# Five pairs of split-weight buffers and seven raw slots in place of three and eleven

## The chip, the cores and the metric

The kernel runs on one core of a Trainium2 chip. The metric is the time of one execution on the device in microseconds (us); of each kernel the median of several runs is given. A profiled execution has a span and a trace of every engine: PE (TensorE, matmuls), DVE (VectorE), ACT (ScalarE), POOL (GpSimd) and SP (SyncE, which issues the loads).

## The reference

One layer of a hybrid backbone over 512 latent tokens of 1024 features (and 256 context tokens): a mixer of a bidirectional state-space scan and a pooling group, an output projection, and then a mixture of 32 experts of which each token takes four. The change lies in the last part.

```python
logits = (xt @ router_w + router_b).astype(jnp.float32)
top_val, top_idx = lax.top_k(logits, TOP_K)            # 4 of 32
gates = jax.nn.softmax(top_val, axis=-1)
...
def run_block(args):
    toks, e = args
    hb = x_pad[toks] @ w1[e] + b1[e]                   # 1024 -> 2048
    g_part = jnp.minimum(hb[..., ::2], SWIGLU_LIMIT)
    u_part = jnp.clip(hb[..., 1::2], -SWIGLU_LIMIT, SWIGLU_LIMIT)
    act = g_part * jax.nn.sigmoid(SWIGLU_ALPHA * g_part) * (u_part + 1)
    return act @ w2[e] + b2[e]                         # 1024 -> 1024
...
x = x + g2 * moe_ffn(...)
return rmsnorm(x, final_norm_w)
```

All of it is float32. w1 and w2 of all experts are 384 MB.

## The kernel before, in words

**Splitting.** A float32 product is made of products of rounded parts. A piece of weights of 1024 KB (`raw`, 128 partitions of 2048 numbers) is loaded by SP (line 1064), rounded by ACT into `hi` (line 1076), and the remainder `lo` = raw - hi is taken by DVE (line 1077). PE then multiplies (`prod`, line 1305): the rounded activations with hi, their remainder with hi, and the rounded activations with lo. For an expert with more than 64 token slots these are twelve matmuls of 512 columns a piece. Where 64 slots do, the rounded and the remaining rows lie side by side in one operand, and there are eight.

**Pieces.** The experts are sorted by load into 32 positions p. From p = 2 on, even positions hold a big expert (128 slots falling to 80; p = 16 has two blocks) and odd ones from p = 3 a small one (64 slots). Each expert has eight pieces of w1 and four of w2; there are 384 pieces, numbered here from 0. PE takes w1 of position p in pieces 12p-4 to 12p+3, and then the four of w2 of position p-1. So the last piece of w1 of p = 10 is number 123, and that of p = 11 is 135. Where a big expert's w1 ends is called a big end here, where a small one's ends a small end.

**Between w1 and w2.** When the last product of w1 is done, PE adds the bias (line 1289 for big, 1287 for small experts; the small ones' bias product needs `b2h`, a copy that ACT makes of w1's sums, line 1276). Then ACT takes the sigmoid product `sg` (line 1314), DVE clips into `su` (line 1319) and multiplies into `act` (line 1320), twice, for two halves. PE transposes `act`, and ACT and DVE split the result (`ah`, `al`). `y` (line 1326) is an expert's result; POOL adds it to the sum in DRAM.

**Buffers.** `ring` lists the slots that raw pieces take in turn: seven of the pool `pcat`, two of `strm`, two of `pm`, which comes in when the router's tiles are given up: eleven. `hring` lists the pairs for hi and lo: two in `strm` and one in `pcat` (tag `hl`): three. Before the experts begin, the same memory of `pcat` holds the transposed heads `cat`, five tiles of 1024 KB of which the first three serve the first pair of token blocks and have tag `raw`.

**Order.** A scheduler places each instruction in its engine's program before the run. Each engine works its program off in that order: what stands behind a waiting instruction waits as well. How the scheduler orders su and act against the splits of later pieces is therefore settled before the run.

Of the kernel before, what the change touches and what calls it, by code (L numbers as in the profile page):

```python
# [6 lines left out]
F32R = mybir.dt.float32r  # L7
# [9 lines left out]
P = 128  # L17
D = 1024
KT = D // P
# [78 lines left out]
def mixer_and_moe(tc, a):  # L98
# [18 lines left out]
    strm = tc.alloc_tile_pool(name="strm", bufs=1, side="right")  # L117
# [17 lines left out]
    acc_scr = dram.tile([T, D], F32, name="acc_scr")  # L135
# [29 lines left out]
    halfneg = cst.tile([P, 8], F32, name="halfneg")  # L165
# [5 lines left out]
    phx = tc.alloc_tile_pool(name="phx", bufs=1, side="right", reuse_waits="tile")  # L171
# [64 lines left out]
    for k in range(KT):  # L236
        for h in range(2):
# [7 lines left out]
            with tc.issue_after(wdma.ins):  # L245
                if 2 * k + h in (5, 9):
                    j = k // 2 - 1
# [414 lines left out]
    cat = [([None] * 4, [None] * 4) for _ in range(2)]  # L662
# [120 lines left out]
    pcat = tc.alloc_tile_pool(name="pcat", bufs=1, side="left", reuse_waits="tile")  # L783

    for i, ts in enumerate(cat):
        for j in range(3 + i):
            t = pcat.tile([P, 2, 4, 2 * P], F32R, name=f"cat{i}{j}", tag="raw", bufs=RC)
            ts[0][j], ts[1][j] = t[:, 0], t[:, 1]
    for c in (2, 3):
        pool_cat(c)  # L790
# [36 lines left out]
    strm = tc.alloc_tile_pool(name="strm2", bufs=1, side="right", reuse_waits="tile")  # L827
    phx = tc.alloc_tile_pool(name="phx2", bufs=1, side="right", reuse_waits="tile")
# [216 lines left out]
    turn = [0, 0]  # L1045
    loads = [0]
    own = [(strm, SR)]
    ring = [(pcat, RC)] * 3 + [(strm, SR)] * SR + [(pcat, RC)] * (RC - 3)
    hring = [(strm, "hi", "lo", SH)] * SH + [(pcat, "hl", "hl", 2)]

    def after(i, j, how, why):
        tc.add_manual_dep(i.ins, j.ins.name, mybir.DependencyInfo(how, mybir.DependencyReason.DATA), reason=why)
# [75 lines left out]
    xgs = [pc.tile([P, D], F32, name=f"xg{i}") for i in range(2)]  # L1128
    for t in xgs:
        PO.memset(t, 0.0)  # L1130
    lead = []
# [10 lines left out]
    for pr in range(2):  # L1142
# [7 lines left out]
        for c in cs_:  # L1150
            route(c)
            normed(c)
            table(c)

    psa = moe(tc, a, c_, cst, psa, psb, phx, pc, pd, g2, b1h, b2h, msum[:, NT - 1, :], gate, rkm, tab, *first[0], table_out,
              acc_scr, halfneg, ring, ring_raw, ring_load, ring_split, w1_piece, w1_pair, w2_pair, gather, transposed, xgs,
              lead)
    pc.release()
    phx.release()
# [27 lines left out]
RAW, HLB = 6, 3  # L1187


RC = 7  # L1190
SR = 2
RX = 2
SH = 2
# [7 lines left out]


def moe(tc, a, c_, cst, psa, psb, phx, pc, pd, g2, b1h, b2h, msum, gate, rkm, tab, ixa, last, table_out, acc_scr, halfneg,
        ring, raw, load, split, w1_piece, w1_pair, w2_pair, gather_, transposed_, xgs, lead):
    nc = tc.nc
    SC, VE, PO, PE, SP = nc.scalar, nc.vector, nc.gpsimd, nc.tensor, nc.sync
    ident = c_("ident")
# [16 lines left out]
    pd.release()  # L1224
    pm = tc.alloc_tile_pool(name="pm", bufs=1, side="right", reuse_waits="tile")
    ring += [(pm, RX)] * RX
    psa.release()
    psa = tc.alloc_tile_pool(name="psa2", bufs=1, space=PSUM, side="left", reuse_waits="tile")

# [371 lines left out]
    def half(dt_=F32):  # L1601

        if not spare.get(dt_):
            t = raw()
            t = t if dt_ is F32 else t.bitcast(dt_)
            spare[dt_] = [t[:, 0:D], t[:, D:]]
        return spare[dt_].pop(0)

    marks = half(F32R)
    place = marks[:, 0:NT * P].rearrange("p (c t) -> p c t", c=NT)  # L1610
    unit = marks[:, NT * P:(NT + 1) * P]
    for c in range(NT):
# [42 lines left out]
    i = None  # L1655
    for c in range(NT):
        for j in range(2):
            for t in (yh, yl):
# [4 lines left out]
                i = x  # L1663
# [19 lines left out]
    with tc.For_i(0, nf, 1) as _:  # L1683
# [38 lines left out]
        for c in range(NT):  # L1722
            t = half()
# [32 lines left out]
```

## Time and profile before

| | |
|---|---|
| runs | 1802.0, 1802.69, 1810.48 us; median 1802.69 |
| profiled execution | 1804.47 us, its span 1802.7 us |
| mean granted clock of PE | 0.964 |
| PE busy | 1635.2 us (91%) |
| DVE busy | 1541.8 us (86%) |
| ACT busy | 1168.1 us (65%) |
| POOL busy | 621.0 us (34%) |
| read from memory | 508.78 MB, 292 GB/s over the span |

The profiled execution is 1.8 us above the median. Of its span the weights of the experts take the stretch from about 580 to 1765 us. Shares over the whole span mix the mixer, the router and the experts; what the change touches is read from the experts' stretch.

### The profile page before, as it was taken

The page shows a single profiled execution, that of the slowest core. Times are in us where ns is not written, and L with a number is a line of the kernel's source. Part 1 is how long each engine was busy: PE and PEld are TensorE (multiplying, and loading weights), DVE is VectorE, ACT ScalarE, POOL GpSimd, SP SyncE. Part 2 cuts the span into 40 slices and gives each one's busy share as a digit, 9 for nine tenths or more (in the row PEclk, how much of TensorE's full clock was granted, in tenths as well). Part 3 has the DMA queues.
Part 4 walks back from the last instruction along what each step waited for, and adds up shares of the span by engine and source line. Part 5 has one row for each costly group of instructions (what it writes and reads, how often), then busy time and mean ns, then how long its engine had stood idle before and what let it go on. Part 6 is the DMA issues. An engine that isn't in the chain of part 4 may idle for free. (4 is left out here: it accounts for less than half of the span.)

```text
span 1802.7 us, 21388 instructions
## 1 busy us (share of the span) xinstructions
PE 1635.2 (91%) x7371; PEld 1197.1 (66%) x7371; DVE 1541.8 (86%) x1491; ACT 1168.1 (65%) x1204; POOL 621.0 (34%) x288
## 2 busy tenths in 40 slices
PE   6998889998899799999999999998999998999985
PEld 2776667676677577767667667676666666666653
DVE  7767888987878989999989998966899999999994
ACT  6445336556643467787777877755778777787773
POOL 1303456779210102242540531501053363313303
PEclk8999899999999889999999999999999999999996
DMA  9646443223577779999999999985899999999953
GB/s 350 200 127 206 150 154 105 101 82 106 191 249 304 258 289 365 363 388 384 362 388 392 356 380 401 351 304 197 341 385 384 380 365 365 390 374 374 384 222 102
DMA packets 138561, 521.53 MB, mean 289 GB/s; under 512 B 14919, under 2 KB 45063, under 8 KB 106704
## 3 DMA queue, kind: packets, MB, share of 16 engines
q1 hardware_dynamic: 125446, 490.39, 71.6%
q0 software_dynamic: 6880, 16.79, 4.0%
q10 hardware_dynamic: 6122, 12.94, 2.1%
q8 instruction: 59, 0.97, 0.2%
q14 instruction: 54, 0.44, 0.1%
HBM read 508.78 MB, written 18.37 MB: 292 GB/s over the span
## 5 line engine op out<-in xcount | busy, mean ns | idle before, releaser
L1077 DVE TENSOR_TENSOR lo<-raw,hi 128x2048 fp32r<-128x2048 f32 x398 | 897.4, 2283 | 88.5 <-ACT hi L1076 85.5
L1076 ACT ACTIVATE hi<-raw 128x2048 fp32r<-128x2048 f32 x398 | 752.0, 1915 | 180.7 <-PE A L1305 106.7
L1328 POOL DMA_INDIRECT acc_scr<-y,ixi x32 | 239.9, 7498 | 531.2 <-DVE y L1326 450.8
L1305 PE MATMUL A<-lo,xh 128*128 128x512 f32 (+3 forms) x1072 | 310.9, 407 | 37.5 <-DVE lo L1077 32.8
L1305 PE MATMUL A<-hi,xh 128*128 128x512 f32 (+3 forms) x1072 | 304.4, 400 | 7.0 <-ACT hi L1076 3.8
L1305 PEld LDWEIGHTS A<-lo,xh 128*128 128x128 f32 (+3 forms) x1072 | 184.3, 181 | 126.9 <-DVE lo L1077 80.0
L1305 PEld LDWEIGHTS A<-hi,xh 128*128 128x128 f32 (+3 forms) x1072 | 192.2, 182 | 62.8 <-ACT hi L1076 5.6
L1099 POOL DMA_INDIRECT xg<-h_scr,ixi x30 | 114.7, 3823 | 269.4 <-PE S L1109 150.2
L1305 PE MATMUL S<-lo,ah 128*128 128x512 f32 (+3 forms) x512 | 165.8, 404 | 15.4 <-DVE lo L1077 15.3
L1305 PE MATMUL S<-hi,ah 128*128 128x512 f32 (+3 forms) x512 | 165.6, 403 | 3.8 <-DVE ah L1112 3.8
L1305 PE MATMUL A<-hi,xl 128*128 128x512 f32 (+3 forms) x544 | 153.8, 396 | 0.0
L1305 PEld LDWEIGHTS S<-lo,ah 128*128 128x128 f32 (+3 forms) x512 | 90.5, 183 | 49.8 <-DVE lo L1077 24.2
L1305 PEld LDWEIGHTS A<-hi,xl 128*128 128x128 f32 (+3 forms) x544 | 95.0, 175 | 31.4
L1305 PEld LDWEIGHTS S<-hi,ah 128*128 128x128 f32 (+3 forms) x512 | 92.6, 184 | 33.2 <-DVE ah L1112 4.0
L228 ACT ACTIVATE hi<-raw 128x1024 fp32r<-128x1024 f32 (+1 forms) x73 | 75.9, 1045 | 40.0 <-PE A L355 14.3
L231 DVE TENSOR_TENSOR lo<-raw,hi 128x1024 fp32r<-128x1024 f32 (+1 forms) x59 | 77.8, 1322 | 18.6 <-ACT hi L228 17.4
L1305 PE MATMUL S<-hi,al 128*128 128x512 f32 (+3 forms) x272 | 86.2, 396 | 0.0
L630 ACT ACTIVATE row<-row,nb 128x128 f32<-128x128 f32 x192 | 59.5, 389 | 37.4 <-POOL row L626 37.3
L336 PE MATMUL A<-hx,hi 128*128 128x512 f32 x160 | 65.8, 411 | 3.4 <-DVE at L378 2.1
L338 PE MATMUL A<-hx,lo 128*128 128x512 f32 x160 | 66.2, 414 | 0.0
L337 PE MATMUL A<-hx,hi 128*128 128x512 f32 x160 | 65.2, 408 | 0.0
L378 DVE SCALAR_TENSOR_TENSOR at<-A,cw,at 128x510 f32<-128x510 f32 (+1 forms) x80 | 57.8, 740 | 5.9 <-ACT at L374 5.4
(452 smaller groups left out, 2476.1 us busy)
## 6 DMA issues: line engine op xcount, KB each, us to landing
raw<-in_w_dram SPq DMA_DIRECT2D x384, 1024.0 KB
raw<-in_w_in_dram SPq DMA_DIRECT2D x36, 512.0 KB
mraw<-in_w_mod_dram SPq DMA_DIRECT2D x32, 512.0 KB
raw<-in_w_out_dram SPq DMA_DIRECT2D x14, 1024.0 KB
row<-cs_scr ACTq DMA_DIRECT2D x32, 384.0 KB
raw<-in_w_mod_dram SPq DMA_DIRECT2D x16, 512.0 KB
raw<-in_w_in_dram SPq DMA_DIRECT2D x16, 384.0 KB
xt<-in_x_dram SPq DMA_DIRECT2D x4, 512.0 KB
```

Of the source, the lines that this page charges most:

```text
L228: SC.activation(hi, r, AF.Copy)
L231: e.tensor_tensor(lo, r, hi.bitcast(F32), op=ALU.subtract)
L336: PE.matmul(lat, lhsT=hi[:, k, :], rhs=row_of(hxh, k), start=(k == 0), stop=False)
L337: PE.matmul(lat, lhsT=hi[:, k, :], rhs=row_of(hxl, k), start=False, stop=False)
L338: newest[0] = PE.matmul(lat, lhsT=lo[:, k, :], rhs=row_of(hxh, k), start=False, stop=(k == KT - 1))
L378: VE.scalar_tensor_tensor(ac[:, u:v], src[:, u + o:v + o], cw[:, j, ct:ct + 1], ac[:, u:v], op0=ALU.mult, op1=ALU.add)
L630: SC.activation(row[:, h, :], row[:, h, :], AF.Exp, bias=nb[:, c, i:i + 1])
L1076: ia = SC.activation(hi, r, AF.Copy)
L1077: i = VE.tensor_tensor(lo, r, hi.bitcast(F32), op=ALU.subtract)
L1099: PO.indirect_dma_start(out=t[0:m, :], out_offset=None, in_=h2_scr, in_offset=bass.IndirectOffsetOnAxis(ap=col[0:m, :], axis=0), bounds_ch ...
L1305: PE.matmul(bk[0:n, :], lhsT=u[:, k, 0:n], rhs=v[:, j * 512:(j + 1) * 512], start=(k == 0 and i == 0), stop=((last or m == LT and k == KT ...
L1328: PO.indirect_dma_start(out=acc_scr, out_offset=bass.IndirectOffsetOnAxis(ap=icol[0:m, :], axis=0), in_=y[0:m, :], in_offset=None, bounds_ ...
```

## The change

The second pair's transposed heads (`cat1`, four tiles) get a tag of their own, `hq`, with four slots, and the raw slots in `pcat` go from seven to three, so the memory is the same. When the experts begin, `hring` is extended by two entries that take hi and lo from the four `hq` slots: five pairs in place of three. The ring of raw slots has five entries until `pm` comes in (nine before) and seven then (eleven before). `marks`, which serves the final sum, moves from a half of a raw slot to the tile `al`. Line numbers after the first edit move by one to four: 1077 becomes 1079, 1076 becomes 1078, 1319 becomes 1323, 1320 becomes 1324, 1314 becomes 1318.

```diff
--- before.py
+++ after.py
@@ -784,7 +784,8 @@
 
     for i, ts in enumerate(cat):
         for j in range(3 + i):
-            t = pcat.tile([P, 2, 4, 2 * P], F32R, name=f"cat{i}{j}", tag="raw", bufs=RC)
+            tag, n = (("raw", RC), ("hq", HQ))[i]
+            t = pcat.tile([P, 2, 4, 2 * P], F32R, name=f"cat{i}{j}", tag=tag, bufs=n)
             ts[0][j], ts[1][j] = t[:, 0], t[:, 1]
     for c in (2, 3):
         pool_cat(c)
@@ -1045,8 +1046,9 @@
     turn = [0, 0]
     loads = [0]
     own = [(strm, SR)]
-    ring = [(pcat, RC)] * 3 + [(strm, SR)] * SR + [(pcat, RC)] * (RC - 3)
+    ring = [(pcat, RC)] * RC + [(strm, SR)] * SR
     hring = [(strm, "hi", "lo", SH)] * SH + [(pcat, "hl", "hl", 2)]
+    more_h = [(pcat, "hq", "hq", HQ)] * (HQ // 2)
 
     def after(i, j, how, why):
         tc.add_manual_dep(i.ins, j.ins.name, mybir.DependencyInfo(how, mybir.DependencyReason.DATA), reason=why)
@@ -1153,7 +1155,7 @@
             table(c)
 
     psa = moe(tc, a, c_, cst, psa, psb, phx, pc, pd, g2, b1h, b2h, msum[:, NT - 1, :], gate, rkm, tab, *first[0], table_out,
-              acc_scr, halfneg, ring, ring_raw, ring_load, ring_split, w1_piece, w1_pair, w2_pair, gather, transposed, xgs,
+              acc_scr, halfneg, ring, (hring, more_h), ring_raw, ring_load, ring_split, w1_piece, w1_pair, w2_pair, gather, transposed, xgs,
               lead)
     pc.release()
     phx.release()
@@ -1187,7 +1189,8 @@
 RAW, HLB = 6, 3
 
 
-RC = 7
+RC = 3
+HQ = 4
 SR = 2
 RX = 2
 SH = 2
@@ -1201,7 +1204,7 @@
 
 
 def moe(tc, a, c_, cst, psa, psb, phx, pc, pd, g2, b1h, b2h, msum, gate, rkm, tab, ixa, last, table_out, acc_scr, halfneg,
-        ring, raw, load, split, w1_piece, w1_pair, w2_pair, gather_, transposed_, xgs, lead):
+        ring, hring, raw, load, split, w1_piece, w1_pair, w2_pair, gather_, transposed_, xgs, lead):
     nc = tc.nc
     SC, VE, PO, PE, SP = nc.scalar, nc.vector, nc.gpsimd, nc.tensor, nc.sync
     ident = c_("ident")
@@ -1224,6 +1227,7 @@
     pd.release()
     pm = tc.alloc_tile_pool(name="pm", bufs=1, side="right", reuse_waits="tile")
     ring += [(pm, RX)] * RX
+    hring[0].extend(hring[1])
     psa.release()
     psa = tc.alloc_tile_pool(name="psa2", bufs=1, space=PSUM, side="left", reuse_waits="tile")
 
@@ -1606,7 +1610,7 @@
             spare[dt_] = [t[:, 0:D], t[:, D:]]
         return spare[dt_].pop(0)
 
-    marks = half(F32R)
+    marks = phx.tile([P, KT, P], F32R, name="marks", tag="al", bufs=1).rearrange("p k t -> p (k t)")
     place = marks[:, 0:NT * P].rearrange("p (c t) -> p c t", c=NT)
     unit = marks[:, NT * P:(NT + 1) * P]
     for c in range(NT):
```

The scheduler's order changes with it. DVE's program around the end of w1 of p = 10 (112 slots, last piece 123), before; the run of nine lo ends with piece 125:

```order
L1077 TENSOR_TENSOR lo<-raw,hi 128x2048 x9
L1319 TENSOR_SCALAR su<-A 112x512
L1320 SCALAR_TENSOR_TENSOR act<-sg,su 112x512
L1077 TENSOR_TENSOR lo<-raw,hi 128x2048
L1319 TENSOR_SCALAR su<-A 112x512
L1077 TENSOR_TENSOR lo<-raw,hi 128x2048
L1320 SCALAR_TENSOR_TENSOR act<-sg,su 112x512
L1077 TENSOR_TENSOR lo<-raw,hi 128x2048
L1326 SCALAR_TENSOR_TENSOR y<-S,gtp,g_4096 64x512
```

The same place after the change; the run of seven ends with piece 124:

```order
L1079 TENSOR_TENSOR lo<-raw,hi 128x2048 x7
L1323 TENSOR_SCALAR su<-A 112x512
L1324 SCALAR_TENSOR_TENSOR act<-sg,su 112x512
L1323 TENSOR_SCALAR su<-A 112x512
L1079 TENSOR_TENSOR lo<-raw,hi 128x2048
L1324 SCALAR_TENSOR_TENSOR act<-sg,su 112x512
L1079 TENSOR_TENSOR lo<-raw,hi 128x2048 x3
L1330 SCALAR_TENSOR_TENSOR y<-S,gtp,g_4096 64x512
```

The first su stood behind the lo of the second piece past w1 and the second su behind the third; now both stand behind the lo of the first piece past w1, with no lo between them.

DVE's program around the end of w1 of p = 11 (64 slots, last piece 135), before; the run of seven lo ends with piece 137:

```order
L1077 TENSOR_TENSOR lo<-raw,hi 128x2048 x7
L1319 TENSOR_SCALAR su<-A 64x512
L1320 SCALAR_TENSOR_TENSOR act<-sg,su 64x512
L1077 TENSOR_TENSOR lo<-raw,hi 128x2048
L1319 TENSOR_SCALAR su<-A 64x512
L1077 TENSOR_TENSOR lo<-raw,hi 128x2048
L1320 SCALAR_TENSOR_TENSOR act<-sg,su 64x512
```

And after; the run of five ends with piece 136:

```order
L1079 TENSOR_TENSOR lo<-raw,hi 128x2048 x5
L1323 TENSOR_SCALAR su<-A 64x512
L1324 SCALAR_TENSOR_TENSOR act<-sg,su 64x512
L1079 TENSOR_TENSOR lo<-raw,hi 128x2048
L1323 TENSOR_SCALAR su<-A 64x512
L1079 TENSOR_TENSOR lo<-raw,hi 128x2048
L1114 TENSOR_TENSOR xh<-S,xh 128x8x64
L1324 SCALAR_TENSOR_TENSOR act<-sg,su 64x512
```

The first su stood two lo past w1's end, the second three; now they stand one and two past it.

ACT's program at the same end of p = 11, before (the run of six ends with piece 136):

```order
L1076 ACTIVATE hi<-raw 128x2048 x6
L1276 ACTIVATE b2h<-A 64x1024
L1076 ACTIVATE hi<-raw 128x2048
L1314 ACTIVATE sg<-A 64x512
L1276 ACTIVATE b2h<-A 64x1024
L1076 ACTIVATE hi<-raw 128x2048
```

After (the run of five ends with piece 136):

```order
L1078 ACTIVATE hi<-raw 128x2048 x5
L1280 ACTIVATE b2h<-A 64x1024
L1318 ACTIVATE sg<-A 64x512
L1280 ACTIVATE b2h<-A 64x1024
L1078 ACTIVATE hi<-raw 128x2048
```

The hi of piece 137 stood between the first copy b2h and sg; now it stands behind sg and the second b2h. In PE's program the twelve transposes for act and the next tokens stood behind the hi products of piece 138 and now stand ahead of those of piece 137.

Over all positions, the number of lo past w1's end that stand ahead of the first and second su goes as follows. Big ends of p = 8, 10, 12, 14, 24, 26 and 28: 2 and 3 before, 1 and 1 now; p = 30: 2 and 2, now 1 and 1. p = 4, 6 and 22: 3 and 4, now 1 and 1. p = 2 and p = 18: 3 and 3, 3 and 5, now 5 and 5, 5 and 7. p = 20: 3 and 4 in both. Small ends of p = 7, 9, 11, 13, 15, 25 and 27: 2 and 3, now 1 and 2; p = 23: 3 and 4, now 1 and 2; p = 5 and 21: 4 and 6, now 1 and 2. p = 19: 4 and 6, now 6 and 8. p = 3, 29 and 31 keep theirs.

## Rows read from the trace of the kernel before

**Rows 1.** A window of 50 us: busy us (instructions) by engine, clock, DMA share, GB/s.

```profile
1000.00:1050.00 50.00, 48.53 (x213) 34.59 (x211) 47.05 (x29) 37.41 (x25) 18.27 (x4) 1.00 1.01 385
```

**Rows 2.** Section 5 of the page: the two splitting operations.

```profile
L1077 DVE TENSOR_TENSOR lo<-raw,hi 128x2048 fp32r<-128x2048 f32 x398 | 897.4, 2283 | 88.5 <-ACT hi L1076 85.5
L1076 ACT ACTIVATE hi<-raw 128x2048 fp32r<-128x2048 f32 x398 | 752.0, 1915 | 180.7 <-PE A L1305 106.7
```

**Rows 3.** Waits of the whole span.

```profile
ACT hi L1076 <- PE A L1305: 106.7, 102, 4.1
...
PE A L1305 <- DVE lo L1077: 32.8, 38, 1.5
```

**Rows 4.** SP's queue: the waits ahead of its loads.

```profile
SPq L1064 <- DVE lo L1077: 891.8, 361, 20.0
```

**Rows 5.** Timeline of PE: first bias products of experts in positions 4, 6, 8 and 10.

```profile
773.36 0.74 PE L1289 MATMUL A<-b1h,sel 64*128 64x512 f32 x4
...
842.44 0.74 PE L1289 MATMUL A<-b1h,sel 64*128 64x512 f32 x4
...
910.34 0.74 PE L1289 MATMUL A<-b1h,sel 64*128 64x512 f32 x4
...
980.31 0.72 PE L1289 MATMUL A<-b1h,sel 64*112 64x512 f32 x4
```

**Rows 6.** Timeline of DVE: the ends of positions 6 and 10.

```profile
843.12 2.29 DVE L1077 TENSOR_TENSOR lo<-raw,hi 128x2048 fp32r<-128x2048 f32 x1 [0.47 <-ACT hi L1076]
...
978.67 2.29 DVE L1077 TENSOR_TENSOR lo<-raw,hi 128x2048 fp32r<-128x2048 f32 x1 [0.48 <-ACT hi L1076]
981.69 0.69 DVE L1319 TENSOR_SCALAR su<-A 112x512 f32<-112x512 f32 x1 [0.73 <-ACT sg L1314]
...
983.98 2.29 DVE L1077 TENSOR_TENSOR lo<-raw,hi 128x2048 fp32r<-128x2048 f32 x1 [0.87 <-ACT hi L1076]
986.19 0.68 DVE L1319 TENSOR_SCALAR su<-A 112x512 f32<-112x512 f32 x1
...
992.37 0.74 DVE L1326 SCALAR_TENSOR_TENSOR y<-S,gtp,g 64x512 f32<-64x512 f32 x1 [0.49 <-PE S L1295]
```

**Rows 7.** Timeline of DVE, ACT and PE: the end of position 11.

```profile
1000.23 13.28 DVE L1077 TENSOR_TENSOR lo<-raw,hi 128x2048 fp32r<-128x2048 f32 x6
1015.12 2.29 DVE L1077 TENSOR_TENSOR lo<-raw,hi 128x2048 fp32r<-128x2048 f32 x1 [1.62 <-ACT hi L1076]
...
1012.13 1.02 ACT L1276 ACTIVATE b2h<-A 64x1024 fp32r<-64x1024 f32 x1 [3.23 <-PE A L1305]
1013.18 1.92 ACT L1076 ACTIVATE hi<-raw 128x2048 fp32r<-128x2048 f32 x1
1015.12 0.59 ACT L1314 ACTIVATE sg<-A 64x512 f32<-64x512 f32 x1
1015.73 1.02 ACT L1276 ACTIVATE b2h<-A 64x1024 fp32r<-64x1024 f32 x1
...
1013.34 0.40 PE L1287 MATMUL A<-b1h,slt 128*64 128x512 f32 x1
...
1017.95 0.63 PE L1305 MATMUL S<-lo,ah 128*112 128x512 f32 x2
```

**Rows 8.** The raw tile's last load and split, and two windows near the end.

```profile
L1076 ACT ACTIVATE hi<-raw x398: 1892/1917/1936, 478.3 to 1763.3; 128x2048 fp32r<-128x2048 f32 x199
...
L1064 SPq DMA_DIRECT2D raw<-in_w_dram x384: 327/345/520, 551.3 to 1736.5; - x192
...
1740.00:1745.00 5.00, 4.91 (x22) 3.06 (x21) 3.38 (x3) 3.24 (x3) 0.00 (x0) 1.00 0.29 116
1745.00:1760.00 15.00, 11.52 (x54) 6.98 (x52) 14.96 (x12) 11.70 (x9) 2.21 (x1) 0.97 0.00 0
```

**Rows 9.** Timeline of SP and DVE: the start of the experts' weights.

```profile
551.31 22.22 SPq L1064 DMA_DIRECT2D raw<-in_w_dram  x9
...
572.37 0.15 DVE L897 TENSOR_SCALAR s2s<-s2s 128x1 f32<-128x1 f32 x1 [1.27 <-ACT h L896]
```

## Prediction

> **What bounds the kernel now.** I read the windows first. In the stretch of the experts no engine is idle for long: of 50 us PE is busy 48.5, DVE 47.1, ACT 37.4, and the DMA engines have work all the time, at 385 GB/s [rows 1]. Four averages near full do not name a bound, so I went on to the waits and to the timelines of single experts.
>
> The list of waits shows two opposite ones: hi waits for PE, 106.7 us in 102 pieces, and PE waits for lo, 32.8 us in 38 [rows 3]. They belong to two phases that alternate. A small expert's piece gives PE eight matmuls (0.23 us apart: the 20 from 1013.34 to 1017.95 take 4.61 us [rows 7]), 1.84 us, and the four of the bias in addition once or twice; DVE needs 2.21 us for its lo (six in 13.28 us [rows 7]). A piece of a big expert gives PE twelve matmuls, 2.76 us, again against 2.21. So while PE does w2 and w1 of small experts, DVE is the bound: this runs from a big end to the small end behind it. From there to the next big end PE is the bound, and DVE waits for free pairs (0.47 and 0.48 us ahead of a lo [rows 6]). From the big end of p = 6 to that of p = 8 are 67.90 us, from p = 8 to p = 10 69.97 [rows 5]; 14 such pairs of experts make up most of the stretch.
>
> DVE's run-ahead when a big end comes is what it brings into the phase that it bounds. Two things limit it: the number of pairs, and where su and act stand in DVE's program, since a lo behind su must wait until w1's last product, the bias and sg are done.
>
> **The change, part by part.** Nothing is computed more or less: 398 hi of 1.92 us and 398 lo of 2.28 [rows 2], the same matmuls, the same loads.
>
> *Big ends.* Two more pairs would let DVE be four or five lo ahead. But the program that the change shows puts both su behind the first lo past the end. The lo of the second piece, which ran while w1 ended (from 978.67 to 980.9; the bias came at 980.31 [rows 5, 6]), now waits behind both su. At p = 10 I walk it through with the times of before: su at 981.69, act, and the second su take some 2 us, to 983.8; the next lo needs its hi, which stands behind both sg, so it starts at 983.98 as piece 126 did (before, the second su came behind that one, at 986.19). Then lo 125, act, lo 126 to 128: 4 x 2.21 + 0.6 = 9.4 us, so y can start at 993.4 where it started at 992.37, and y waited 0.49 there for PE, which now has its lo later as well; with that wait kept in part it is 994.1. So 1.0 to 1.7 us by this walk; 2.2 if nothing gives, one whole lo. A comparison inside the kernel says the same: at p = 6 the lo of the third piece stood ahead of the first su (843.12, over at 845.3 [rows 6]) and DVE had no gap before su; at p = 8, as at p = 10, the second did, and the pair took 69.97 in place of 67.90 us, 2.07 more for one lo less [rows 5]. I take 1.8 us for each lo of run-ahead, between 1.0 and 2.2. Eight big ends lose one (8 x 1.8 = 14.4) and three (p = 4, 6, 22) lose two (3 x 3.6 = 10.8): **25.2 us**, bounds 14 and 31.
>
> *Small ends.* Here the next phase is PE's, so a lo that comes late costs only what PE waits. Walked through for p = 11 [rows 7]: the bias comes at 1013.34 and is over at 1014.45 with its latency; sg now follows at once, to 1015.04, then the second b2h, 1.02, to 1016.1, and only then hi of piece 137, 1.92, to 1018.0, and its lo, 2.28, to 1020.3, where it was over at 1017.4. PE took this lo up at 1017.95, but now has the twelve transposes ahead of it, some 1.2 us by an estimate of 0.1 each, under half of a matmul's 0.23 (so it comes to it at 1019.2). PE waits 1.1 us, and 0.2 at piece 138, behind the second su: 1.3 us. Below lies nothing (if PE comes later than I think), above 2.2 (a whole lo). Eight small ends go from two or three lo ahead to one: 8 x 1.3 = **10.4 us**. The two whose su stood four lo late (p = 5, 21) paid for that too: from p = 4 to p = 6, with such an end between, are 69.08 us, 1.2 more than from p = 6 to p = 8 [rows 5]; what is gained there cancels the 1.3, and I count nothing. Bounds of the sum: 0 and 22.
>
> *Where su moved the other way.* At p = 2 and p = 18 both su now stand five lo past the end, two more: here the five pairs are used. 4 x 1.8 = **7.2 us** gained, bounds 0 and 8.8.
>
> *Raw slots.* A load waits for the lo that frees its slot (891.8 us in 361 loads is SP's waiting for lo [rows 4], none of it on the path). With four slots fewer it is issued four lo later, 4 x 2.21 = 8.8 us to 4 x 2.76 = 11. What margin is there shows the end of the stream: the last load is issued at 1736.5, the DMA engines have nothing more by 1745, and the last hi runs at 1763.3 [rows 8]. So a load lands within 8.5 us and then lies 18 us. Of these 7 remain: nothing, while landing takes under some 11 us (seven pieces at 2.21 less one hi and one lo, 4.2).
>
> *Start.* Nine loads went out at once from 551.31 [rows 9], now five until `pm` is there. The splits that stand ahead of the router's last tile block get some of their instructions moved past its s2s (572.37 [rows 9]); I estimate one lo's delay for half a chain, **1 us**, from the 2.2 of a lo, between -3 (PE's first products come together without gaps) and +8 (four loads missing at 2.21 each, nearly all shown).
>
> *marks* is written after the last split, beside sums that wait for the results in DRAM: nothing; were it in the way, a fill of a tile, under 1 us.
>
> Sum: 25.2 + 10.4 - 7.2 + 1 = **29.4 us** on 1804.5 of the profiled execution; less the 1.8 by which that is above the median, **1832 us**. With all bounds at their low ends it is +2 (1805), at their high ends +62 (1865).
>
> **The rivals.** *Faster: the pairs bind, not the order.* The 106.7 us in which hi waits for PE [rows 3] are a wait for free pairs; if DVE gets to be four lo ahead at a big end, eight ends win two lo and three win one, 19 x 1.8 = 34 us, 1769. It decides at one place: whether the lo of the second piece past a big end is over when DVE takes up the first su. Against it stands the program: a lo behind su cannot. The waits of hi fall into PE's phase, and PE has no gap there. The Trainium skill, page "Perfetto Trace Analysis", section "Optimization Strategy", speaks for this rival: the same gap over and over on the engine that should be saturated can mean too few buffers for the next tile. The gap is there, but by the trace it is ACT's and DVE's in the phase in which PE is the saturated one; by the rule the kernel would come to the 1769 of this rival, by the rows to 1832.
>
> *No change.* If y and the products behind it have slack that I do not see, the big ends cost 0.4 each and the small ones nothing: 14 x 0.4 - 7.2 + 1 = about 0, 1802. For it speaks that DVE waits 0.5 us ahead of lo after lo in PE's phase, so a late lo is caught up; against it that the pairs from p = 6 and p = 8 differ by 2.07 us and nothing caught that up.
>
> *Much slower: raw slots bind.* The DMA engines are busy in all of the window, at 385 GB/s [rows 1], while six lo in 13.28 us ask for 474. If landing takes 12 us rather than 8.5 in DVE's phase, each of its twelve pieces takes 1/7 us more for every us over 11, 14 phases x 12/7 = 24 us, on top of the sum: 1856. Against it stand the 7 us that remain.
>
> **How the numbers follow.** My forecast has 0.66, faster 0.12, no change 0.14, raw slots 0.08. The likeliest one's own range is 1805 to 1865; few of its costs will stand at one end together. The range that should hold the time 8 times in 10 is 1796 to 1852: below it lies the faster rival (0.12), above it the raw slots' (0.08) and little else. A measurement of this kernel can tell about 0.5%, 9 us: 1793.7 to 1811.7 is no change. To that go the rival of that name and 0.04 of the forecast: faster 0.12, same 0.18, slower 0.70.
>
> **What the profile after would show.** Right: before su at a big end DVE idle some 3 us for sg; PE waiting for lo about 1 us behind a small end; 71 to 73 us from one big end to the next, and gains only at p = 2 and 18; hi's waits for PE shorter, as pairs are free; no wait of hi for a load; the same busy time of DVE and ACT. Wrong: the lo of the second piece past a big end over before su (then the first rival), hi waiting for raw (then the last), pairs of experts still at 68 to 70 us (then no change), or a start that is later or earlier by more than 8 us.

## The result and the profile after

The change made the kernel slower: 1859.70 us (median of 1857.81, 1859.46, 1859.95, 1860.50) against 1806.33 (now four runs: 1802.0, 1802.69, 1809.97, 1810.48), a ratio of 1.0294 with a 95% interval of 1.0261 to 1.0327. The direction was forecast, the size was not: 29 us were forecast and 53 measured, and the time lies above the range. The profiled execution's span is 1858.0 us, where it was 1802.7. The busy times of DVE and ACT did not grow with it (1539.9 us, 1541.8 before, and 1154.3, 1168.1 before); PE's went from 1635.2 to 1652.2 us with the same instructions.

Waits over the whole span of the kernel after (us in total, times, longest):

```profile
DVE su L1323 <- ACT sg L1318: 66.2, 24, 4.5
...
ACT hi L1078 <- PE A L1309: 45.1, 31, 8.2
...
PE A L1309 <- DVE lo L1079: 40.2, 41, 1.8
...
PE S L1309 <- DVE lo L1079: 30.6, 27, 1.6
...
ACT hi L1078 <- DMA raw<-in_w_dram: 15.6, 3, 11.0
```

The waits of hi for PE have more than halved, from 106.7 to 45.1 [rows 3]: pairs are free, as they should be. In their place su waits 66.2 us for sg, 24 times (10.0 us, 12 times, before), and PE's waits for lo grew (32.8 to 40.2 us in the products of w1, 15.3 to 30.6 in those of w2). hi waited for a load three times in 384 pieces.

The starts of the bias at the ends of p = 4, 6, 8 and 10, on PE:

```profile
778.15 0.74 PE L1293 MATMUL A<-b1h,sel 64*128 64x512 f32 x4
...
852.58 0.74 PE L1293 MATMUL A<-b1h,sel 64*128 64x512 f32 x4
...
928.02 0.73 PE L1293 MATMUL A<-b1h,sel 64*128 64x512 f32 x4
...
1001.88 0.72 PE L1293 MATMUL A<-b1h,sel 64*112 64x512 f32 x4
```

From one big end to the next pass 74.4, 75.4 and 73.9 us, where it was 69.1, 67.9 and 70.0 [rows 5].

DVE at the end of p = 10 after the change:

```profile
987.70 11.09 DVE L1079 TENSOR_TENSOR lo<-raw,hi 128x2048 fp32r<-128x2048 f32 x5
1003.26 0.69 DVE L1323 TENSOR_SCALAR su<-A 112x512 f32<-112x512 f32 x1 [4.46 <-ACT sg L1318]
1003.98 0.69 DVE L1324 SCALAR_TENSOR_TENSOR act<-sg,su 112x512 f32<-112x512 f32 x1
1004.78 0.69 DVE L1323 TENSOR_SCALAR su<-A 112x512 f32<-112x512 f32 x1
1005.54 2.29 DVE L1079 TENSOR_TENSOR lo<-raw,hi 128x2048 fp32r<-128x2048 f32 x1
1007.75 0.68 DVE L1324 SCALAR_TENSOR_TENSOR act<-sg,su 112x512 f32<-112x512 f32 x1
1008.36 6.69 DVE L1079 TENSOR_TENSOR lo<-raw,hi 128x2048 fp32r<-128x2048 f32 x3
1016.39 0.74 DVE L1330 SCALAR_TENSOR_TENSOR y<-S,gtp,g 64x512 f32<-64x512 f32 x1 [1.35 <-PE S L1299]
```

Here the new order is seen at work. The run of lo ends at 998.8 with piece 124, and DVE stands 4.46 us idle ahead of su until sg has come. Both su, act, and then lo 125: it begins 3.66 us after the bias (1001.88), as in the forecast's walk (983.98 - 980.31 = 3.67 [rows 5, 6]). y begins 14.5 us after the bias, where before it was 12.1 (992.37 - 980.31), 2.4 us later; the walk had 1.0 to 1.7.

The same from the small end of p = 11 to the next big end, first before, then after:

```profile
1050.04 0.72 PE L1289 MATMUL A<-b1h,sel 64*112 64x512 f32 x4
...
1037.87 0.40 PE L1291 MATMUL A<-b1h,slt 128*64 128x512 f32 x1
...
1076.15 0.72 PE L1293 MATMUL A<-b1h,sel 64*112 64x512 f32 x4
```

36.7 us before (from 1013.34 [rows 7]), 38.3 after.

Where the 55 us went, stretch by stretch, from the starts of the bias products on PE (the first is a time, the others are differences, the last reaches to the end of the span), for both kernels and the experiments below:

| kernel | end of p = 2 | to p = 4 | to p = 16 | to p = 18 | to p = 22 | to p = 30 | to the end |
|---|---|---|---|---|---|---|---|
| before | 703.5 | 69.9 | 420.5 | 104.7 | 136.9 | 274.9 | 92.2 |
| after | 710.7 | 67.4 | 450.8 | 109.1 | 131.8 | 292.4 | 95.7 |
| e1 | 705.4 | 68.9 | 452.2 | 105.1 | 137.5 | 292.7 | 94.8 |
| e2 | 709.7 | 67.4 | 435.3 | 110.3 | 132.0 | 282.7 | 94.7 |
| e3 | 701.4 | 69.8 | 444.3 | 110.7 | 137.8 | 289.0 | 93.6 |
| e4 | 709.3 | 67.4 | 419.4 | 109.3 | 132.0 | 273.8 | 92.7 |
| e5 | 711.2 | 67.4 | 423.2 | 109.0 | 130.0 | 276.8 | 95.4 |
| e6 | 711.6 | 67.4 | 415.2 | 110.0 | 129.9 | 267.8 | 92.7 |
| e7 | 700.7 | 69.8 | 415.1 | 105.6 | 136.5 | 272.0 | 91.3 |
| e8 | 710.0 | 67.4 | 450.8 | 109.1 | 131.9 | 292.5 | 95.8 |
| e9 | 709.2 | 69.1 | 412.7 | 110.1 | 132.5 | 270.1 | 93.0 |
| e9b | 712.0 | 69.1 | 415.2 | 111.6 | 131.9 | 268.6 | 92.4 |
| e10 | 706.9 | 69.1 | 436.1 | 108.7 | 133.1 | 281.6 | 98.5 |
| e11 | 711.2 | 67.4 | 436.5 | 108.7 | 129.9 | 285.2 | 97.2 |

After less before: 7.2 at the start, -2.5, **30.3** from p = 4 to 16, 4.4 at the expert with two blocks, -5.1 where su moved later, **17.5** from p = 22 to 30, and 3.5 at the end.

The experiments are read from single ends too, taken from the same starts: from a big end to the small end behind it (8 to 9, 10 to 11), and from a small end to the next big one (5 to 6, 9 to 10, 11 to 12).

| kernel | 8 to 9 | 10 to 11 | 5 to 6 | 9 to 10 | 11 to 12 |
|---|---|---|---|---|---|
| before | 33.2 | 33.0 | 34.9 | 36.7 | 36.7 |
| after | 35.5 | 36.0 | 38.8 | 38.4 | 38.3 |
| e2 | 33.4 | 33.2 | 38.4 | 38.6 | 38.5 |
| e3 | 35.2 | 34.0 | 38.9 | 38.4 | 38.4 |
| e4 | 33.3 | 31.0 | 35.5 | 35.6 | 38.5 |
| e5 | 33.4 | 33.2 | 36.4 | 36.4 | 36.4 |
| e6 | 33.3 | 31.0 | 35.5 | 35.7 | 36.4 |
| e7 | 31.8 | 31.7 | 37.7 | 36.7 | 36.7 |
| e11 | 35.5 | 35.3 | 36.4 | 36.5 | 36.4 |

### The profile page after: what moved, and what is told of

Its sections match the earlier page's. It is cut to its first block, busy times and chain, and to the rows that moved or that the text cites. A ratio compares the mean times of both kernels' runs of the same rounds, so it can differ in the third digit from the quotient of the medians.

```text
span 1858.0 us, 21394 instructions
## 1 busy us (share of the span) xinstructions
PE 1652.2 (89%) x7371; PEld 1203.4 (65%) x7371; DVE 1539.9 (83%) x1491; ACT 1154.3 (62%) x1204; POOL 595.8 (32%) x288
## 5 line engine op out<-in xcount | busy, mean ns | idle before, releaser
L1079 DVE TENSOR_TENSOR lo<-raw,hi 128x2048 fp32r<-128x2048 f32 x398 | 893.0, 2282 | 75.5 <-ACT hi L1078 74.4
L1078 ACT ACTIVATE hi<-raw 128x2048 fp32r<-128x2048 f32 x398 | 738.7, 1911 | 96.4 <-PE A L1309 45.1
L1309 PE MATMUL A<-lo,xh 128*128 128x512 f32 (+3 forms) x1072 | 312.8, 408 | 43.3 <-DVE lo L1079 40.2
L1101 POOL DMA_INDIRECT xg<-h_scr,ixi x30 | 142.8, 4761 | 574.7 <-PE S L1121 349.6
L1309 PE MATMUL A<-hi,xh 128*128 128x512 f32 (+3 forms) x1072 | 310.4, 404 | 9.1 <-DVE su L1323 4.8
L1332 POOL DMA_INDIRECT acc_scr<-y,ixi x32 | 187.1, 5847 | 300.3 <-DVE sel L1271 176.6
L1309 PEld LDWEIGHTS A<-lo,xh 128*128 128x128 f32 (+3 forms) x1072 | 189.0, 184 | 129.7 <-DVE lo L1079 81.1
L1309 PE MATMUL S<-lo,ah 128*128 128x512 f32 (+3 forms) x512 | 173.4, 421 | 31.0 <-DVE lo L1079 30.6
L1309 PE MATMUL S<-hi,ah 128*128 128x512 f32 (+3 forms) x512 | 170.6, 414 | 7.5 <-DVE ah L1114 4.8
L1309 PEld LDWEIGHTS S<-lo,ah 128*128 128x128 f32 (+3 forms) x512 | 93.0, 190 | 69.9 <-DVE lo L1079 46.3
L1309 PEld LDWEIGHTS A<-hi,xl 128*128 128x128 f32 (+3 forms) x544 | 96.2, 177 | 31.7
L1318 ACT ACTIVATE sg<-A 64x512 f32<-64x512 f32 (+4 forms) x66 | 37.4, 591 | 126.1 <-PE A L1293 107.7
L1323 DVE TENSOR_SCALAR su<-A 64x512 f32<-64x512 f32 (+4 forms) x66 | 45.1, 683 | 67.6 <-ACT sg L1318 66.2
L336 PE MATMUL A<-hx,hi 128*128 128x512 f32 x160 | 65.7, 411 | 4.0 <-DVE at L378 2.5
```

The lines of the kernel that those rows point to most:

```text
L336: PE.matmul(lat, lhsT=hi[:, k, :], rhs=row_of(hxh, k), start=(k == 0), stop=False)
L1078: ia = SC.activation(hi, r, AF.Copy)
L1079: i = VE.tensor_tensor(lo, r, hi.bitcast(F32), op=ALU.subtract)
L1101: PO.indirect_dma_start(out=t[0:m, :], out_offset=None, in_=h2_scr, in_offset=bass.IndirectOffsetOnAxis(ap=col[0:m, :], axis=0), bounds_ch ...
L1309: PE.matmul(bk[0:n, :], lhsT=u[:, k, 0:n], rhs=v[:, j * 512:(j + 1) * 512], start=(k == 0 and i == 0), stop=((last or m == LT and k == KT ...
L1318: SC.activation(g, v[:, :, 0], AF.Gelu_apprx_sigmoid)
```

## The experiments

The theory: sg and su stand too early in ACT's and DVE's programs, so that the splits behind them stand still at each end of w1; the buffers themselves cost nothing. Its rivals: seven raw slots starve the splits; the five pairs cost by their place; the start.

**e1, the slots without the pairs.**

```diff
-    more_h = [(pcat, "hq", "hq", HQ)] * (HQ // 2)
+    more_h = []
```

> Seven raw slots as in the change, but three pairs as before; the four tiles of the second pair of heads stay unused after that. The order on ACT and DVE at the ends of w1 becomes that of the change all the same (one lo past a big end ahead of both su), so the scheduler's new order goes with the fewer slots. If the place of sg and su is what costs: 1850 to 1870 us, and hi waits for no load from p = 4 on. If the five pairs cost, by their place or otherwise: 1800 to 1815.

Measured: 1859.77 us (1855.85 to 1861.58), 1.0309 (1.0284 to 1.0333) of the kernel before. With three pairs the kernel is as slow as with five, and its order at the big ends from p = 6 on is the same. So the two more pairs change nothing in sum, and the order that costs came with the fewer raw slots. They do not leave every stretch alone: with five pairs the end of p = 2 comes 5.3 us later than in e1 and the expert with two blocks takes 4.0 us longer, and from p = 18 to 22 5.7 are gained. In e1's table row the stretches from 4 to 16 and 22 to 30 are those of the change.

**e2, the order put back.** In ring_split each hi and lo is kept; in swiglu sg and su are tied between two of them, without a wait, for the scheduler alone. BIG and SMALL give, for the two halves, how many hi stand ahead of sg and how many lo ahead of su.

```diff
+            LOS.append((ia, i))
+            for k, x, behind in PLACE.pop(len(LOS) - 1, ()):
+                after(*((x, LOS[-1][k]) if behind else (LOS[-1][k], x)), mybir.DependencyClass.NoSync, "where it stands")
...
+            for k, x, n0 in ((0, ia, at[0]), (1, i, at[1])) if at else ():
+                for n, behind in [(n0, True)] + [(n0 + j, False) for j in range(1, 5)]:
+                    if n >= len(LOS):
+                        PLACE.setdefault(n, []).append((k, x, behind))
+                    elif behind:
+                        after(x, LOS[n][k], "where it stands")
...
+BIG, SMALL = ((2, 2), (2, 3)), ((2, 2), (3, 3))
```

> The change with its seven slots and five pairs, but with sg and su of p = 4 to 15 and 21 to 30 placed as most of them stood before: at big ends sg behind the second hi past w1's end and su behind the second and third lo, at small ends sg and su behind the second and third. If the place of sg and su is what costs: 1816 us (1808 to 1824), and 69 to 70 us from one big end to the next. If seven raw slots starve the splits: 1852 to 1862, as the change.

Measured: 1833.76 us (1833.36 to 1835.02), 1.0167 (1.0148 to 1.0186). Neither number of the expectation: 26 us came back and 18 did not. The second table says which: from the big end of p = 10 to the small one behind it 33.2 us pass, as before (33.0), but from the small end of p = 11 to the next big one 38.5, as in the change (38.3; before 36.7). ACT and PE at the small end of p = 11 in e2:

```profile
1027.36 1.02 ACT L1289 ACTIVATE b2h<-A 64x1024 fp32r<-64x1024 f32 x1 [1.36 <-PE A L1300]
1028.41 1.91 ACT L1078 ACTIVATE hi<-raw 128x2048 fp32r<-128x2048 f32 x1
...
1030.38 0.72 PE L1318 MATMUL S<-hi,ah 128*112 128x512 f32 x2 [0.34 <-ACT hi L1078]
...
1032.70 0.72 PE L1318 MATMUL S<-lo,ah 128*112 128x512 f32 x2 [1.14 <-DVE lo L1079]
```

The hi of piece 137 still stands behind the second b2h (1027.36), which waits for PE's first bias products. PE then waits 0.34 us for that hi and 1.14 for its lo. Before, hi stood ahead of this copy, at 1013.18 [rows 7]. So the place of su was not what the small end loses by.

**e3, the change's order in the kernel before** (eleven slots, three pairs; the same code as e2):

```diff
+BIG, SMALL = ((1, 1), (1, 1)), ((1, 1), (2, 2))
```

> The kernel before, eleven slots and three pairs, with sg and su of p = 4 to 15 and 21 to 30 placed as the change has them (one piece past a big end, one and two past a small end). If the place is what costs: 1850 us (1842 to 1858), 73 to 75 us from one big end to the next. If the buffers are what costs: 1800 to 1812.

Measured: 1849.76 us (1846.36 to 1851.64), 1.0254 (1.0231 to 1.0278). The big ends of p = 10 and 12 in e3:

```profile
991.59 0.72 PE L1298 MATMUL A<-b1h,sel 64*112 64x512 f32 x4
...
1063.98 0.72 PE L1298 MATMUL A<-b1h,sel 64*112 64x512 f32 x4
```

72.4 us between them, in place of 69.7, with not one buffer changed. The order alone makes the kernel 46 us slower; the change's own loss over the two long stretches (p = 4 to 16 and 22 to 30) is 47.8, and e3's there is 37.9. What the other 10 us are was not tried; e3 ties sg and su alone.

**e4, DVE four pieces ahead at big ends** (with the change's buffers):

```diff
+BIG, SMALL = ((4, 4), (4, 4)), ((2, 2), (3, 3))
```

> As e2_order_restored, but at big ends sg and both su stand behind the fourth hi and lo past w1's end, which only five pairs allow. If DVE's run-ahead into the stretch that it bounds is worth some 1.9 us a piece, as in the prediction: 1785 us (1775 to 1800), 66 to 67 us from one big end to the next. If late su delays the transposes for w2, or DVE can not get so far ahead while PE works on the big expert's w1: 1815 or more.

Measured: 1806.08 us (1804.66 to 1806.82), 1.0012 (1.0003 to 1.0022), between the two numbers of the expectation and 27.7 us less than e2. Not all of that is run-ahead. At p = 10 and 12 and from 22 on the stretch behind a big end takes 2.2 us less than in e2 (31.0 in place of 33.2), for two pieces more; at p = 4 to 8 and 14 it takes as long as in e2. There the stretch behind the next small end is shorter, 35.6 in place of 38.6 from p = 9 to 10. At p = 5, 7, 9 and 15 the scheduler had put the hi of the second piece ahead of the second b2h by itself. ACT at p = 5 in e4:

```profile
808.46 1.92 ACT L1078 ACTIVATE hi<-raw 128x2048 fp32r<-128x2048 f32 x1
...
811.96 1.02 ACT L1289 ACTIVATE b2h<-A 64x1024 fp32r<-64x1024 f32 x1
```

At p = 11, 13 and from 21 to 27 it left hi behind the copy, and 38.5 us pass there as in e2. So e4 mixes two causes; e5 and e6 part them.

**e5, the small ends' hi as well**: e2, and the second b2h tied behind the hi of the second piece.

```diff
+                r = rest([two[1]])
+                if at[0]:
+                    PLACE.setdefault(at[0][0], []).append((0, r, True))
```

> As e2_order_restored, and at the small ends ACT's second b2h copy stands behind the second hi past w1's end, as it did before (in e2 the hi stood behind both copies, and 38.5 us passed from a small end to the next big one, where before it were 36.7). If that hi is what the small ends lose: 1816 us (1811 to 1821), and 36.7 us again. If the small ends lose by the transposes that PE has earlier, or by the buffers: 1830 to 1835.

Measured: 1814.11 us (1812.1 to 1816.31), 1.0049 (1.0033 to 1.0066), 19.7 us less than e2. The small end of p = 11 and the big end of p = 12 in e5:

```profile
1021.60 0.40 PE L1300 MATMUL A<-b1h,slt 128*64 128x512 f32 x1
...
1057.99 0.72 PE L1302 MATMUL A<-b1h,sel 64*112 64x512 f32 x4
```

36.4 us, in place of 38.5 in e2; it is 2.0 to 2.2 less at each of the ten small ends where the copy moved. That hi is what the small ends lost. What is left of e5 above the kernel before, 9 us, lies in the table at the start (7.7), at the expert with two blocks (4.3), in the two long stretches (4.6) and the end (3.2), less what p = 4 and 18 to 22 gain.

**e6, the best order for five pairs**: e4 and e5 together, and SP's reads of the experts' numbers behind the load of piece 12.

```diff
+        with tc.issue_after(LOADS[12].ins):
+            return nc.values_load(permi[0][0:1, p:p + 1], engines=[mybir.EngineType.SP], min_val=0, max_val=E - 1)
...
+BIG, SMALL = ((4, 4), (4, 4)), ((2, 2), (3, 3))
```

> Seven slots and five pairs with the order as in e5, but sg and su behind the fourth piece at big ends (as e4), and SP reads the experts' numbers (permi) only behind the load of piece 12. If five pairs are worth something once the order lets DVE run ahead: 1787 us (1778 to 1798), below both kernels. If what e4 gained at big ends was only paid at small ends: 1800 or more.

Measured: 1796.26 us (1795.01 to 1797.4), 0.9951 (0.9934 to 0.9967): quicker than both kernels. The big end of p = 10, the small of 11 and the big of 12:

```profile
986.10 0.72 PE L1305 MATMUL A<-b1h,sel 64*112 64x512 f32 x4
...
1017.06 0.39 PE L1303 MATMUL A<-b1h,slt 128*64 128x512 f32 x1
...
1053.46 0.72 PE L1305 MATMUL A<-b1h,sel 64*112 64x512 f32 x4
```

31.0 and 36.4 us, 67.4 in all. e6 has the small ends of e5, so the step from e5, 17.9 us for two pieces more at eleven big ends, gives the price of run-ahead: 0.8 us a piece, less than the 1.9 of the expectation. It is 1.1 at p = 10, 12 and from 22 on, and under half of that at p = 4 to 8 and 14. In this order hi waits for loads as well, from p = 4 on:

```profile
ACT hi L1079 <- DMA raw<-in_w_dram: 12.6, 10, 2.9
```

The ten waits lie ahead of the big ends of p = 6 to 14. With nine slots (e9) there is none from p = 4 on.

**e7, three pairs and eleven slots with a set order**: the kernel before and the code of e5.

```diff
+BIG, SMALL = ((3, 3), (3, 4)), ((2, 2), (3, 3))
```

> The kernel before, eleven slots and three pairs, with sg and su behind the third (and fourth) piece at big ends and behind the second and third at small ends, as it had them at p = 6 and 7 alone, where the pair took 67.9 us in place of 69.7. If the place sets the time: 1787 us (1782 to 1797), as good as the five pairs. If p = 6 was quick for another cause: 1800 to 1808.

Measured: 1793.15 us (1792.69 to 1797.63), 0.9942 (0.9925 to 0.996), the lowest median of all, though its interval overlaps those of e6 and e9. The same three ends in e7:

```profile
976.02 0.72 PE L1298 MATMUL A<-b1h,sel 64*112 64x512 f32 x4
...
1007.72 0.39 PE L1296 MATMUL A<-b1h,slt 128*64 128x512 f32 x1
...
1044.41 0.72 PE L1298 MATMUL A<-b1h,sel 64*112 64x512 f32 x4
```

31.7 and 36.7 us, 68.4 in all. Here and from p = 22 to 30 five pairs with a set order win 1.0 us a pair of experts over three with a set order; over all of p = 4 to 16 the two are equal (415.2 and 415.1), and at the start five pairs with seven slots lose 11 us (711.6 against 700.7 at the end of p = 2).

**e8, the start's loads ahead of the reads**: the change, and the reads as in e6.

> The change, with SP's reads of the experts' numbers (permi) only behind the load of piece 12. In the change two loads that PE needs for the first expert stand behind eight such reads, which wait for permi until 617.4 us. If that is the start's loss: 1852 us (1848 to 1857), the first big end at 628 to 634 in place of 641 us. If the slots come free no earlier than that: 1857 to 1862, the first big end at 640.

Measured: 1858.99 us (1857.55 to 1863.29), 1.0304 (1.0285 to 1.0323): no different from the change. SP's wait at the start and the first big end in e8:

```profile
SPq L1066 <- DVE permi L1456: 10.3, 1, 10.3
...
640.30 0.74 PE L1296 MATMUL A<-b1h,sel 64*128 64x512 f32 x4
```

With the reads moved behind it a load still waits 10.3 us for the same event of DVE, and the first big end comes at 640.3, as in the change. The reads were not what held the loads up.

**e9 and e9b, four pairs and nine slots**, with sg and su behind three or four pieces at big ends:

```diff
-RC = 3
-HQ = 4
+RC = 5
+HQ = 2
...
-            tag, n = (("raw", RC), ("hq", HQ))[i]
+            tag, n = ("raw", RC) if i == 0 or j < RC - 3 else ("hq", HQ)
...
-    ring = [(pcat, RC)] * RC + [(strm, SR)] * SR
+    ring = [(pcat, RC)] * 3 + [(strm, SR)] * SR + [(pcat, RC)] * (RC - 3)
```

> Between the two: four pairs and nine raw slots (seven loads can go out before the router's tiles are given up), sg and su behind the third (and fourth) piece at big ends, and small ends as in e5. If each part costs what the runs so far say, the start lies between (first big end 628 to 636 us; 625 to 628 with nine, 638 to 642 with five) and a pair of experts takes 67.3 to 68 us: 1789 us (1784 to 1796), as e7 with three pairs. If the fourth pair is worth as much as a lo of run-ahead: 1778 to 1784.

> As e9, but sg and both su behind the fourth piece at big ends. With four pairs the fourth hi must wait until the last piece of w1 is used, so sg, which stands behind it, comes 2 us late: 1790 us (1785 to 1798), not quicker than e9. If run-ahead alone decides: 2 to 10 us quicker than e9.

Measured: e9 1795.95 us (1794.52 to 1798.55), 0.9952 (0.9933 to 0.9971); e9b 1799.62 (1792.96 to 1802.74), 0.9963 (0.9947 to 0.998), from which it can not be told apart. From p = 4 to 16 e9 is the quickest of all (412.7), but the start did not come between. ACT's wait at the start and the first big end in e9:

```profile
ACT hi L1078 <- DMA raw<-in_w_dram: 4.2, 1, 4.2
...
640.89 0.74 PE L1302 MATMUL A<-b1h,sel 64*128 64x512 f32 x4
```

Seven loads ahead leave the first big end at 640.9, as five do (e1 637.9, after 641.2); nine give 627.8. It is no matter of so much a load.

**e10, four pairs and nine slots in the scheduler's own order.**

> Four pairs and nine slots, as the scheduler orders them: at seven big ends one and two lo past the end ahead of the two su, at small ends two and three, and the hi of the second piece ahead of the second copy b2h as before. If the place is what costs, only the big ends lose, 7 x 2 us, and the start some 3: 1818 us (1810 to 1826). If the count of buffers costs by itself: 1830 or more, or 1805 or less.

Measured: 1837.78 us (1835.81 to 1839.49), 1.0190 (1.0170 to 1.0209), 20 us above the first number of the expectation and in the range of the second, in which the count of buffers costs by itself. But e9, with the same buffers and a set order, takes 1795.95, so 42 us of it are order. Its small ends are whole (36.7 us), and eight of its big ends lose some 3 each (36.1 at p = 10), although DVE's order has one and two lo ahead of the two su. ACT and DVE at the big end of p = 10:

```profile
990.14 1.09 ACT L1318 ACTIVATE sg<-A 112x512 f32<-112x512 f32 x2 [7.97 <-PE A L1293]
991.11 7.32 ACT L1078 ACTIVATE hi<-raw 128x2048 fp32r<-128x2048 f32 x4
...
993.06 2.29 DVE L1079 TENSOR_TENSOR lo<-raw,hi 128x2048 fp32r<-128x2048 f32 x1 [0.88 <-ACT hi L1078]
```

ACT has both sg ahead of the hi of the second piece, so its lo waits 0.88 us for that, between the two su. One lo more ahead of the second su is worth nothing when its hi stands behind sg.

**e11, the small ends alone put right**: the change's big ends and the code of e5.

```diff
+BIG, SMALL = ((1, 1), (1, 1)), ((2, 2), (3, 3))
```

> The change with its big ends as they are, but the small ends placed as in e5 (hi of the second piece ahead of the second b2h, su behind the second and third lo). e2 and e5 put 26 us to the big ends and 20 to the small. If the two add up independently: 1840 us (1836 to 1845), 36.4 us from a small end to the next big one. If the late lo at small ends only matter together with the late ones at big ends: 1850 or more.

Measured: 1836.03 us (1832.11 to 1837.87), 1.0170 (1.0146 to 1.0193). 23.7 us for the small ends by themselves, 19.7 behind e2: the two losses add up, nearly.

## Why the prediction was right in direction and wrong in size

Of the 26 us by which the loss of the profiled spans (55.3) exceeds the forecast (29.4), some 13 are the small ends', 6 the start's, 4 the expert's with two blocks and 3 lie behind the last small end.

**Right, in the two long stretches: the order, not the buffers.** e3 shows it for 37.9 of 47.8 us without any change of a buffer, and e1 without the pairs. What the prediction did not see is which part of the change moved the order: it spoke of the pairs that the order can not use; e1 shows that the seven slots bring that order, with three pairs as with five. That the scheduler does so because it counts on later data is an argument, and was not tested.

**Right: big ends.** The forecast was 25.2 us; e2 gave 25.9 back, and before and after differ by 26.9 over the eleven stretches. By the single ends it is 2.3 to 3.0 at p = 8 to 14 (35.5 and 36.0 us to the small end in place of 33.0 to 33.2), where 1.8 was taken; y is 2.4 us late there and not 1.0 to 1.7. Of the ends that lose two lo, p = 4 and 22 lose 1.5 and 2.0 and p = 6 4.6, where 3.6 was taken, and p = 30 loses 0.5 for its one. That these errors cancel is luck; the sum is closer than the price of a lo was known.

**Right: p = 2 and 18.** 7.2 us were forecast; 2.5 and 5.1 were gained in these stretches. e1 has 68.9 and 137.5 there (before 69.9 and 136.9), so most of this gain came with the pairs.

**Wrong: the term of the small ends, 10.4 us.** It measured 19.7 (e2 to e5) to 23.7 (after to e11), and 24.9 as before and after differ over these stretches. Two steps failed: the walk at p = 11, whose 1.3 us was taken for eight ends, and the nothing that was set for p = 5 and 21. The walk's mechanism was right, in the kernel after step by step:

```profile
1036.67 1.02 ACT L1280 ACTIVATE b2h<-A 64x1024 fp32r<-64x1024 f32 x1 [3.85 <-PE A L1309]
1038.99 0.59 ACT L1318 ACTIVATE sg<-A 64x512 f32<-64x512 f32 x1 [1.30 <-PE A L1291]
1039.61 1.02 ACT L1280 ACTIVATE b2h<-A 64x1024 fp32r<-64x1024 f32 x1
1040.65 1.92 ACT L1078 ACTIVATE hi<-raw 128x2048 fp32r<-128x2048 f32 x1
...
1044.95 0.72 PE L1309 MATMUL S<-lo,ah 128*112 128x512 f32 x2 [1.13 <-DVE lo L1079]
```

The second b2h, and the hi behind it, come as walked; PE waits 1.13 us for the lo. But to the next big end it is 1.6 us longer (38.3 against 36.7), not 1.1 + 0.2. The wait of 1.13 us is the only one in this stretch; what the other 0.5 is, the runs do not show. Over the eight ends the loss is 1.5 to 2.1 at six of them and 2.9 and 4.3 at p = 7 and 23, 17.6 in sum for 10.4. And the two ends at p = 5 and 21 do pay: their stretches are 3.9 and 3.6 us longer, and e11 takes 36.4 us at either, as at the others, where the change takes 38.8 and 38.3. (From p = 20 to 22 the change loses nothing in sum, as forecast, since the stretch ahead is shorter by as much; e11 takes 66.4 us there and both kernels 68.3.)

**Wrong: the start, 1 us.** The end of p = 2 comes 7.2 us late, and the first big end 13.3 (641.2 against 627.8). The start was priced at -3 to +8, and 1 was taken, half a lo's delay in the router's chain; the missing loads stood only in the upper bound. The end of p = 2 keeps within that bound, the first big end does not. PE, ACT and SP there:

```profile
629.79 2.08 PE L1309 MATMUL A<-hi,xh 128*128 128x512 f32 x4 [2.44 <-ACT hi L1078]
...
627.83 9.12 ACT L1078 ACTIVATE hi<-raw 128x2048 fp32r<-128x2048 f32 x5 [4.01 <-DMA raw<-in_w_dram]
...
SPq L1066 <- DVE permi L1452: 10.3, 1, 10.3
```

ACT waits 4.0 us for a load and PE 2.4 for that hi, after the products of the pieces at hand are used up. From 622 to 637 us, around that wait, PE's mean granted clock is 0.54, where the kernel before has 1.00 from 613 to 626; and 2.0 of the 13.3 us lie ahead of the first product, for which the gathered tokens land later (598.75 against 596.79 us). A load waits for DVE up to the write of permi. e8 takes away the one cause that I had put down for it, the reads in SP's queue, and nothing changes; e9 and e10 with seven loads ahead have their first big end as late (640.9 and 638.7). The first expert's w1 has eight pieces, and nine slots hold them all; that the lack of any one of the eight sets the loss fits all runs, but was not tested by itself (eight loads ahead were not run).

**Not in the sum: the expert with two blocks, +4.4 us.** The prediction set this place to nothing. From its first bias to that of p = 18, before and then after (times busy of PE, PEld, DVE, ACT and POOL; the third number from the end is the granted clock):

```profile
1193.90:1298.60 104.70, 93.44 (x395) 67.49 (x394) 69.68 (x50) 59.77 (x48) 12.40 (x6) 0.95 0.68 247
...
1229.00:1338.10 109.10, 95.94 (x395) 70.43 (x394) 74.20 (x52) 62.97 (x50) 7.52 (x5) 0.89 0.69 255
```

PE stands idle 1.9 us longer, and its 395 matmuls take 2.5 us more at a lower mean clock. All ten runs with four or five pairs take 108.7 to 111.6 us here. Of those with three, before, e1 and e7 take 104.7 to 105.6; e3 takes 110.7, with a wait of PE for su of 3.73 us that no other has. So the loss goes with the pairs, by the order that the scheduler makes here with them or otherwise; which instruction decides was not tried.

**Not in the sum: behind the last small end, +3.1 us.** From the bias of p = 31 to the end the kernel before takes 59.8 us and the change 62.9. All runs with three pairs take 59.8 to 60.3 and all with more 62.7 to 63.5. The new place of *marks* is not it, since e1 has that as well (60.3). What it is was not tried.

**The rivals.** The measured time lies nearest to the 1856 of the rival that raw slots bind, but not for its cause. In the change raw slots do not starve the splits: hi waited for a load three times, 15.6 us in all, of which 15.0 at the start (the longest, 11.0, ahead of the first piece, where ACT was idle for 12.6 us before too). e6 and e9 run their long stretches faster than the kernel before with seven and nine slots, though seven begin to bind in e6, with its ten waits. The condition of the faster rival was not met in the change, where the lo of the second piece stands behind both su. Where the order meets it (e4, e6), the stretch behind a big end shrinks to 31.0 us at p = 10, so pairs are worth something. But the price of 1.8 us a piece was too high for a gain (0.8 from e5 to e6), e6 came to 1796 and not to 1769, and e7 gets as far with three pairs. No change: the pairs of experts from p = 4 to 14 took 73.9 to 75.4 us in place of 67.9 to 70.0, so the late lo were not caught up. By the Trainium skill's page "Perfetto Trace Analysis" (section "Optimization Strategy"), which was named for it, the same gap repeating on the engine that should be saturated can mean too few buffers. Here the gap lay on ACT (hi waiting for PE, 106.7 to 45.1 us); it closed and the kernel became slower, and it became quicker, to 1793 us, with the three pairs it had. The same page of the Trainium skill (section "Tensor Engine Instruction (MATMUL, LD_WEIGHTS)") says that ACT and DVE take their instructions strictly in order. The trace agrees: lo 125 stood behind su while DVE was idle for 4.46 us, and e3 lost 46 us by the order alone.

## What to carry to other kernels

When a buffer count is changed in a kernel whose order a scheduler sets, the first thing to compare is the order, and on every engine in the chain: a lo placed well on DVE is worth nothing when its hi stands behind a waiting instruction on ACT (e2, e10). A gap that repeats is worth closing only on the engine that bounds the stretch in which it lies; ask first what stands next in that engine's program. Tie the few instructions that matter in place by hand and either buffer plan becomes quicker than both kernels were, by some 0.5% of the kernel before; with that done, the plan with three pairs was no worse than those with four and five.

## What the runs showed of the hardware that had not been expected

At five of the ten big ends from p = 4 to 14 and from 22 to 28 of the kernel after (p = 10, 12, 22, 24 and 28), PE came out of its wait for lo at half speed. PE at the end of p = 10, and windows around it and behind the end of p = 8 (the third number from the end is the granted clock):

```profile
1007.89 1.12 PE L1309 MATMUL S<-lo,ah 128*128 128x512 f32 x2 [1.59 <-DVE lo L1079]
1008.81 1.05 PE L1309 MATMUL S<-hi,ah 128*128 128x512 f32 x2
...
1001.90:1007.80 5.90, 4.09 (x19) 2.37 (x18) 4.33 (x5) 5.17 (x5) 0.00 (x0) 1.00 0.81 335
1007.80:1011.40 3.60, 3.51 (x9) 2.63 (x10) 3.60 (x4) 3.11 (x2) 0.00 (x0) 0.53 0.64 223
928.00:943.00 15.00, 12.82 (x57) 8.73 (x57) 12.31 (x9) 10.73 (x8) 0.00 (x0) 1.00 0.83 324
```

The granted clock of the 3.6 us behind the wait is 0.53, the lower of PE's two levels (1.2 in place of 2.4 GHz); the eight matmuls there lie 0.43 us apart in place of 0.23. Before it PE had been busy for 4.1 of 5.9 us. At p = 8 the same order ran at 1.00. The price is small here: 36.0 us from that big end to the small one, against 35.5 at p = 8 and 35.3 at p = 10 in e11, where the clock held. It is larger where PE is the bound: behind the small end of p = 7 the mean clock was 0.66 for 5 us after a wait of 1.12 us, and 39.8 us passed to the next big end, against 38.4 behind p = 9 with the same order. Over the two long stretches the mean clock was 0.99 and 0.98, and 1.00 in both before, so by these two prices an estimated 4 us of the change's 47.8 there are the clock's.
